# Decoder step on one core: the weight loads run eight products ahead instead of seven around one stage boundary

## The chip, the cores and the metric

The kernel runs on one core of one Trainium2 chip. The metric is the time of one execution in device microseconds; three runs of the kernel before gave 2320.79, 2322.99 and 2325.85 us, and the median, 2322.99 us, is its time.

## The reference, cut to what matters

Two layers of a hybrid decoder work on 1024 prompt tokens and 8 sample tokens of width 2048. The first layer is a pooling mixer, the second is sliding-window attention over one shared K/V. All products are in float32. Around the change the second layer is computed:

```python
k_p, v_p = shared_kv(xp, pos_p, w_kv)          # h @ w_kv, rotary on k
z = x @ w_in                                    # queries and gates
q = rope_partial(z[..., :D_ATTN].reshape(B, T, N_HEADS, HEAD_DIM), pos)
o = attn_core(q, kb, vb, q_pos, k_pos, sinks).reshape(B, T, D_ATTN)
y = (o * jax.nn.silu(gate)) @ w_out
return layer_norm(ALPHA * x + y, g_ln, b_ln)
```

## The kernel before, in words

**Stages.** The tokens are cut into two chunks of 512 and 520 columns. The table PHASES (lines 50 to 53) gives the order: input projection of layer one for both chunks, its output projection for both chunks, then `bi` for chunk 0 (fifth stage), `bi` for chunk 1 (sixth), `bo` for both chunks. A `bi` stage projects K/V and then, for eight pairs of heads, queries and gates, and does the attention in between.

**Products.** A projection of 256 output channels is done by Strassen's scheme as seven products of half size (`seven`, line 596). One product is 24 matmuls on TensorE (PE), lines 684 to 686: eight slices of weights, each as high part of the weights by high part of x, high by low, and low by high. So a product needs its weights as two tiles (high, low) and its x as two pairs of tiles. A pair of heads takes 14 products, seven for queries and seven for gates. In the K/V part two runs of seven go side by side (`both`, line 581), and two products in a row use the same x. At the start of a chunk 1 stage three extra matmuls (line 672) are issued first; their PSUM banks are those that the last pair of the stage before still holds.

**What a product costs the other engines.** A weight block (128x1024 float32, 512 KB) is loaded by SyncE (SP) in `load1` (line 285), rounded to its high part by ScalarE (ACT) in `cast_to` (line 505), and the low part is made by VectorE (DVE) in `prep_to` (line 520). Some blocks are sums of others: DVE adds (line 349), and GpSimd (POOL) stores the sum to HBM (line 351) for the second chunk. The x tiles of the next stage are loaded (line 828), cast (line 838) and subtracted (line 847) in the same way, one step of each after a product (`x_tick`). The results leave PSUM by copies of the next product's start (`posts`: lines 623 to 657; line 657 is the last copy of a pair). Attention adds per head: scores on PE (line 1874), a copy and a maximum (1891, 1895), eight exponentials (1910), eight scalings (1923), a transpose on PE (1927), two copies out (1936 on ACT, 1937 on DVE), values on PE (1951), the gate (1960) and its store by POOL (1963). Rotary needs the rows of the other half: four DMAs (`partner`, line 1728), two multiplications (1736) and an addition (1844), and the scores wait for that addition.

**What sets the order.** Everything is written in one stream. `begin` (line 532), called at each product, reads the triple `self.ahead`: weights are loaded up to `a` blocks ahead of the product, cast up to `b` ahead, and made low up to `d` ahead. It is (7, 4, 3) from the start. PE, DVE and ACT keep the order of the source; SP and POOL issue in an order that the tile scheduler chose when the program was built. All engines run in order, so an instruction that waits holds what stands behind it.

**Buffers.** `Mem` (line 139) hands out 54 slots, always the one that was freed longest ago; a slot whose contents are still being stored counts as ten releases younger. A tile is named m, slot, running number (m29_1955 is the 1955th tile, in slot 29). A load into a slot waits for the last reader of what was in it.

**`at(n, f)`** (line 570) runs f at the end of the n-th product from now. In `queries`, at the last pair of heads of chunk 1, `self.ahead` becomes (6, 4, 3), and in the seventh stage it goes back to (7, 4, 3).

Of the kernel before, what the change touches and what calls it, by code (L numbers as in the profile page):

```python
# [190 lines left out]
class Kern:  # L191
# [1918 lines left out]
    def phase_bi(self, c, ps, nxt):  # L2110
        nc = self.nc
        T = CHUNKS[c][1]
        if ps[0] == 0:
            self.kv_open(c)
        if not self.strassen:
            for done in (self.k_done, self.v_done):
                box = {}
                for j in range(2):

                    def take(ps, j=j, done=done, box=box):  # L2120
                        if j == 0:
                            box["s"] = self.mem.full(2 * T)
                        nc.scalar.copy(box["s"].a[:, j * T : (j + 1) * T], ps[:])
                        if j == 1:
                            done(c, box["s"])

                    self.unit(take)
            for t in range(2 * ps[0], 2 * ps[-1] + 2):
                def q_done(ps, t=t):
                    s = self.mem.half(T)  # L2130
                    nc.scalar.copy(s.a[:, :T], ps[:])
                    self.q_done(c, t, s, 1, 4)

                def g_done(ps, t=t):
                    s = self.mem.half(T)
                    nc.scalar.copy(s.a[:, :T], ps[:])
                    self.gate_done(c, t, s, 1)

                self.attend(c, t, 9, 13 if t <= 2 * ps[-1] else 8, 2)
                self.unit(q_done)  # L2140
                if t == 2 * ps[-1] - 1:
                    self.x_begin(nxt)
                self.last = t == 2 * ps[-1] + 1
                self.unit(g_done)
            self.last = False
            return
        if ps[0] == 0:
            pairs = []
            for done in (self.k_done, self.v_done):
                box, z0, z1 = self.two(T)  # L2150
                pairs.append((z0, z1, lambda done=done, box=box: done(c, box["s"])))
            self.both(c, *pairs)

        def queries(p):
            t0 = 2 * p
            if T > TP and p % 4 == 3:
                self.at(2, lambda p=p: self.dec_keys(p // 4))
            for n in range(2):
                t = t0 + n
                at, s1, ticks = (12 + 7 * n, {12: 11, 13: 9}.get(t, 12), SPREAD) if t < 14 else (  # L2160
                    11 + 7 * n, {14: 10, 15: 8}[t], CLOSE
                )
                self.attend(c, t, at, s1, 2, t > 12, ticks)
            if p == ps[-1]:
                self.x_begin(nxt)
                if c == 1:
                    self.ahead = 6, 4, 3
            box, z0, z1 = self.two(T)
            self.pair(c, z0, z1, lambda t0=t0, box=box: self.q_done(c, t0, box["s"], 2, 3))

        def gates(p):
            box, z0, z1 = self.two(T)

            def done():
                self.gate_done(c, 2 * p, box["s"], 2)
                if T > TP and p % 4 == 3:
                    self.decode(c, p // 4)

            self.last = p == ps[-1]
            self.pair(c, z0, z1, done)  # L2180

        for p in ps:
            queries(p)
            gates(p)
        self.last = False
# [296 lines left out]
```

## Time and profile before

| what | value |
|---|---|
| median of three runs | 2322.99 us |
| the profiled execution's own time | 2320.17 us |
| its span, first to last instruction | 2317.9 us |
| mean granted TensorE clock over the span | 0.997 |
| PE, DVE, ACT busy, share of the span | 99%, 84%, 60% |
| DMA over the span | 649.37 MB, 280 GB/s |

All times of the trace are microseconds from the start of the span, in the profiled execution. A row of a timeline has the start, the duration, the engine, the line in the kernel, the operation, the tiles (out<-in, without numbers), the shape and a count; a bracket at its end gives the engine's idle time ahead of it and what is believed to have ended it. SPq marks a DMA that SP issues: the row's duration is that of the issue, not of the transfer. A row of the view of waits has the waiting instruction, the one it waited for, the sum, the count and the longest.

### The profile page before, as it was taken

What the parts mean: (1) busy time and instruction counts of PE and PEld (TensorE: products, weight loads), DVE (VectorE), ACT (ScalarE), POOL (GpSimd) and SP (SyncE); (2) the same over time, 40 slices, a digit from 0 to 9 for tenths busy, and PEclk for the clock granted to TensorE, in tenths of its full rate; (3) what the DMA queues carried; (4) which work ended last, traced back from release to release, by engine and by line L of the source; (5) the groups of instructions that cost most, each with busy time, mean ns of one, the idle gap of its engine ahead of it and who ended that gap; (6) DMA issues with size and microseconds to landing.
All of it is one profiled execution on the core that took longest, in us unless ns stands there. A gap on an engine that the chain in (4) does not pass through costs nothing. (4 is left out here: it accounts for less than half of the span.)

```text
span 2317.9 us, 50529 instructions
## 1 busy us (share of the span) xinstructions
PE 2288.1 (99%) x20417; PEld 2217.7 (96%) x20417; DVE 1943.0 (84%) x2409; ACT 1389.3 (60%) x2548; POOL 191.1 (8%) x360
## 2 busy tenths in 40 slices
PE   9999999999999999999999999999999999999997
PEld 7999999999999999999889999989999999999997
DVE  8888889877878878988979898889877777889797
ACT  5544446544546547655566767685776678556565
POOL 0111110010000000000001111100000000000001
PEclk9999999999999999999999999999999999999999
DMA  7869679999989989999767666777787878799795
GB/s 261 287 242 315 229 245 330 315 309 303 304 302 322 335 284 333 317 392 345 245 234 241 233 234 236 252 259 250 234 252 240 252 230 288 251 360 381 252 330 184
DMA packets 246682, 649.37 MB, mean 280 GB/s; under 512 B 25232, under 2 KB 106032, under 8 KB 246448
## 3 DMA queue, kind: packets, MB, share of 16 engines
q1 hardware_dynamic: 204432, 493.66, 63.8%
q0 software_dynamic: 42016, 152.49, 17.0%
q8 instruction: 159, 2.61, 0.5%
q14 instruction: 75, 0.61, 0.1%
HBM read 463.54 MB, written 173.01 MB: 275 GB/s over the span
## 5 line engine op out<-in xcount | busy, mean ns | idle before, releaser
L684 PE MATMUL pD<-m,m 128*128 128x260 f32 (+1 forms) x5088 | 1441.3, 283 | 4.7 <-ACT pD L623 2.3
L686 PE MATMUL pD<-m,m 128*128 128x260 f32 (+1 forms) x5088 | 1434.7, 282 | 4.9 <-DVE m L520 4.9
L685 PE MATMUL pD<-m,m 128*128 128x260 f32 (+1 forms) x5088 | 1434.7, 282 | 0.0
L684 PEld LDWEIGHTS pD<-m,m 128*128 128x128 f32 x5088 | 959.4, 189 | 13.9 <-issue 6.2
L686 PEld LDWEIGHTS pD<-m,m 128*128 128x128 f32 x5088 | 959.8, 189 | 7.1 <-DVE m L520 7.0
L685 PEld LDWEIGHTS pD<-m,m 128*128 128x128 f32 x5088 | 959.1, 189 | 0.5
L520 DVE TENSOR_TENSOR m<-m,m 128x1024 fp32r<-128x1024 f32 x690 | 833.5, 1218 | 94.7 <-ACT m L505 44.1
L505 ACT CAST m<-m 128x1024 fp32r<-128x1024 f32 x690 | 720.5, 1049 | 249.9 <-DVE m L349 120.3
L349 DVE TENSOR_TENSOR m<-m,m 128x1024 f32<-128x1024 f32 x136 | 166.1, 1222 | 10.2 <-DMA m<-in_wia 5.7
L847 DVE TENSOR_TENSOR m<-m,m 128x1024 fp32r<-128x1024 f32 (+1 forms) x118 | 143.8, 1224 | 7.4 <-ACT m L838 5.8
L838 ACT CAST m<-m 128x1024 fp32r<-128x1024 f32 (+1 forms) x118 | 123.3, 1051 | 11.8 <-DVE m L520 3.5
L657 ACT COPY m<-pD 128x260 f32<-128x260 f32 (+1 forms) x89 | 33.2, 373 | 131.0 <-PE pD L686 131.0
L645 DVE TENSOR_TENSOR m<-pD,m 128x260 f32<-128x260 f32 (+1 forms) x92 | 38.4, 418 | 73.1 <-ACT pD L644 67.2
L1910 ACT ACTIVATE m<-m,sm 128x128 f32<-128x128 f32 x256 | 99.4, 392 | 0.0
L623 ACT ACTIVATE pD<-pD 128x260 f32<-128x260 f32 (+1 forms) x90 | 33.3, 370 | 102.2 <-PE pD L686 102.0
L1179 PE MATMUL pD<-m,m 128*128 128x260 f32 (+1 forms) x528 | 91.5, 323 | 0.0
L712 PE MATMUL pD<-m,m 128*128 128x512 f32 x224 | 89.1, 398 | 0.0
L714 PE MATMUL pD<-m,m 128*128 128x512 f32 x224 | 88.2, 394 | 0.0
L713 PE MATMUL pD<-m,m 128*128 128x512 f32 x224 | 88.1, 393 | 0.0
L1179 PEld LDWEIGHTS pD<-m,m 128*128 128x128 f32 x528 | 79.4, 188 | 8.2
L1923 ACT ACTIVATE m<-m,sm 128x128 f32<-128x128 f32 x256 | 81.8, 391 | 3.8 <-DVE sm L1918 3.4
L632 ACT COPY m<-pD 128x260 f32<-128x260 f32 (+1 forms) x92 | 34.3, 373 | 82.3 <-PE pD L686 82.0
(257 smaller groups left out, 2101.3 us busy)
## 6 DMA issues: line engine op xcount, KB each, us to landing
m<-in_wib SPq DMA_DIRECT2D x132, 512.0 KB
m<-in_wia SPq DMA_DIRECT2D x128, 512.0 KB
m<-swoa SPq DMA_DIRECT2D x64, 512.0 KB
swia<-m POOLq DMA_DIRECT2D x56, 512.0 KB, 4.9
m<-swia SPq DMA_DIRECT2D x56, 512.0 KB
m<-swob SPq DMA_DIRECT2D x56, 512.0 KB
m<-in_wob SPq DMA_DIRECT2D x52, 512.0 KB
m<-in_woa SPq DMA_DIRECT2D x48, 512.0 KB
```

The source lines that it names most:

```text
L349: self.nc.vector.tensor_add(s[out].a[:, :1024], s[x].a[:, :1024], s[y].a[:, :1024])
L505: self.nc.scalar.copy(hi.r[:, :1024], self.stream[self.cast].src().a[:, :1024])
L520: self.nc.vector.tensor_sub(lo.r[:, :1024], s.src().a[:, :1024], hi.a[:, :1024])
L684: nc.tensor.matmul(ps[:, :TH], wh[:, s], h, start=new and k == 0, stop=False, skip_group_check=on)
L685: nc.tensor.matmul(ps[:, :TH], wh[:, s], l, start=False, stop=False, skip_group_check=on)
L686: nc.tensor.matmul(ps[:, :TH], wl[:, s], h, start=False, stop=k == 7, skip_group_check=on)
L712: nc.tensor.matmul(ps[:], wh[:, s], h, start=par == 0 and k == 0, stop=False)
L714: nc.tensor.matmul(ps[:], wl[:, s], h, start=False, stop=par == 1 and k == 7)
L838: self.nc.scalar.copy(h.r[:, :n], s.a[:, :n])
L847: self.nc.vector.tensor_sub(l.r[:, :n], s.a[:, :n], h.a[:, :n])
L1179: nc.tensor.matmul(ps[:, : cs.stop - cs.start], ws[:, s], d[:, cs], start=f0 and k == 0, stop=l0 and k == 3,)
L1910: nc.scalar.activation(x["s3"][:, i, :], x["s3"][:, i, :], AF.Exp, bias=nm[:, i : i + 1], scale=0.125, accum_out=rs[:, i : i + 1],)
```

## The change

In `queries`, at the last pair of heads (p = 7), chunk 0 now also changes the triple: weights are loaded eight blocks ahead. It goes back to seven after 30 more products; 14 of these belong to the last pair, the others are the first of the sixth stage. Casts and low parts stay four and three ahead.

```diff
                 self.x_begin(nxt)
                 if c == 1:
                     self.ahead = 6, 4, 3
+                else:
+                    self.ahead = 8, 4, 3
+                    self.at(30, lambda: setattr(self, "ahead", (7, 4, 3)))
             box, z0, z1 = self.two(T)
```

No matmul, cast, copy or transfer is added or dropped. PE's rows are the same in the same order. What moves is the order of DMAs on SP and POOL, the slots that tiles get, and, in the sixth stage, the steps that sum the next weights (lines 453 to 459), most of them by a product or two.

The first place is SP's queue at the last pair of heads of the fifth stage, up to the first loads for the sixth. in_wib holds query and gate weights of this stage, in_wkv the K/V weights with which the sixth begins, h1 and th1 the x tiles of the sixth; L1728 are the four rotary DMAs of the last queries. Before:

```order
L285 DMA m29_1974_17956<-in_wib 128x1024
L828 DMA m19_1979_18002<-h1_95 128x4x260
L828 DMA m12_1989_18088<-th1_92 128x4x260
L1728 DMA m32_1977_17995<-m23_1962_17784 32x1024 x4
L828 DMA m1_1978_18000<-h1_95 128x4x260
L285 DMA m48_1980_18006<-in_wkv 128x1024
L828 DMA m50_1983_18044<-h1_95 128x4x260
L828 DMA m0_1984_18046<-h1_95 128x4x260
L285 DMA m14_1986_18050<-in_wkv 128x1024
L285 DMA m40_1990_18091<-in_wkv 128x1024
L285 DMA m20_1997_18136<-in_wkv 128x1024
```

and now:

```order
L285 DMA m43_1975_17958<-in_wkv 128x1024
L285 DMA m28_1970_17912<-in_wib 128x1024
L285 DMA m29_1991_18093<-in_wkv 128x1024
L828 DMA m19_1979_18002<-h1_95 128x4x260
L1728 DMA m5_1978_17997<-m46_1963_17786 32x1024 x4
L828 DMA m48_1980_18004<-h1_95 128x4x260
L285 DMA m33_1981_18008<-in_wkv 128x1024
L828 DMA m14_1984_18046<-h1_95 128x4x260
L828 DMA m39_1985_18048<-h1_95 128x4x260
L285 DMA m47_1987_18052<-in_wkv 128x1024
L828 DMA m40_1990_18090<-th1_92 128x4x260
```

Ahead of the rotary DMAs stood one weight load and two x tiles; now two K/V blocks (m43, m29), one block of gate weights and one x tile stand there. Of what follows them, the second K/V block (m14 before, m33 now) is the fifth transfer before and the second now.

The second place is ACT at the same boundary, from the first x cast of the sixth stage to the copy that ends the fifth stage (L657). Before:

```order
L838 CAST m17_1995_18132<-m1_1978_18000 128x1040
L638 COPY m43_1996_18134<-pD_329_17962 128x256
L505 CAST m52_1999_18140<-m48_1980_18006 128x1024
L838 CAST m41_2001_18219<-m19_1979_18002 128x1040
L644 COPY pD_329_17962<-pD_334_18004 128x256
L505 CAST m32_2005_18229<-m14_1986_18050 128x1024
L1923 ACTIVATE m39_1973_17952<-m39_1973_17952,sm_333_17991 128x128 x4
L1891 COPY m29_2006_18261<-pS_215_13088 128x768
L838 CAST m33_2008_18266<-m50_1983_18044 128x1040
L505 CAST m46_2012_18275<-m40_1990_18091 128x1024
L1923 ACTIVATE m39_1973_17952<-m39_1973_17952,sm_333_17991 128x128 x4
L838 CAST m31_2014_18315<-m0_1984_18046 128x1040
```

and now:

```order
L838 CAST m34_1996_18134<-m19_1979_18002 128x1040
L638 COPY m20_1997_18136<-pD_329_17964 128x256
L505 CAST m25_2000_18142<-m43_1975_17958 128x1024
L838 CAST m1_2002_18221<-m48_1980_18004 128x1040
L644 COPY pD_329_17964<-pD_334_18006 128x256
L505 CAST m28_2006_18231<-m33_1981_18008 128x1024
L1923 ACTIVATE m23_1974_17954<-m23_1974_17954,sm_333_17993 128x128 x4
L1891 COPY m50_2007_18263<-pS_215_13088 128x768
L838 CAST m2_2009_18268<-m14_1984_18046 128x1040
L505 CAST m9_2013_18277<-m47_1987_18052 128x1024
L1923 ACTIVATE m23_1974_17954<-m23_1974_17954,sm_333_17993 128x128 x4
L838 CAST m21_2015_18317<-m39_1985_18048 128x1040
```

The operations are the same in the same order (the L657 copy is the next row in both); only the slots differ. The cast of the second K/V block writes m32 before, a slot whose last reader was the rotary addition (L1844), and m28 now, where the seventh block of gate weights lay, read last by its own low part (L520).

The third place is SP at the end of the sixth stage. o0 and to0 are x tiles of the seventh stage, in_wob its weights. Before:

```order
L828 DMA m29_2529_23969<-o0_88 128x4x256
L828 DMA m39_2530_23971<-o0_88 128x4x256
L285 DMA m14_2524_23923<-swib15_140 128x1024
L1728 DMA m28_2527_23962<-m9_2510_23759 32x1040 x4
L285 DMA m42_2531_23975<-in_wib 128x1024
L2010 DMA out_nks<-m27_2506_23713 128x1024
L828 DMA m41_2535_24015<-o0_88 128x4x256
L828 DMA m49_2536_24017<-to0_85 128x4x256
L285 DMA m12_2538_24021<-in_wob 128x1024
L828 DMA m4_2541_24059<-to0_85 128x4x256
L285 DMA m35_2542_24062<-in_wob 128x1024
```

and now:

```order
L828 DMA m11_2533_23973<-o0_88 128x4x256
L828 DMA m52_2534_23975<-o0_88 128x4x256
L285 DMA m40_2528_23927<-swib15_140 128x1024
L285 DMA m23_2542_24025<-in_wob 128x1024
L1728 DMA m47_2531_23966<-m10_2514_23763 32x1040 x4
L285 DMA m53_2535_23979<-in_wib 128x1024
L2010 DMA out_nks<-m20_2510_23717 128x1024
L828 DMA m1_2539_24019<-o0_88 128x4x256
L828 DMA m12_2540_24021<-to0_85 128x4x256
L828 DMA m44_2545_24063<-to0_85 128x4x256
L285 DMA m48_2546_24066<-in_wob 128x1024
L285 DMA m3_2553_24112<-in_wob 128x1024
```

The first in_wob block has moved ahead of the four rotary DMAs; its slot (m23) is one whose contents, an attention output, POOL stores.

## The prediction

> **What bounds the kernel now.** First the page: who is busy.
>
> ```profile
> span 2317.9 us, 50529 instructions
> PE 2288.1 (99%) x20417; PEld 2217.7 (96%) x20417; DVE 1943.0 (84%) x2409; ACT 1389.3 (60%) x2548; POOL 191.1 (8%) x360
> ```
>
> PE is busy for 2288.1 of 2317.9 us, and the change takes no matmul away. All that it can win lies in the remaining 29.8 us and in busy time that runs at a lower clock. The view of PE's waits says where the 29.8 us are (waiting line, who ended the wait, sum, count, longest):
>
> ```profile
> PE pD L686 <- DVE m L520: 4.9, 9, 0.9
> PE pD L672 <- ACT m L657: 4.9, 1, 4.9
> PE pD L684 <- ACT m L657: 1.6, 1, 1.6
> ```
>
> The second row is the only long single wait: 4.9 us, once, at L672. That is the boundary of the fifth and sixth stages, the place of the change. PE's timeline there:
>
> ```profile
> 1506.40 0.28 PE L686 MATMUL pD<-m,m 128*128 128x256 f32 x1
> 1511.60 1.02 PE L672 MATMUL pD<-m,m 128*128 128x260 f32 x3 [4.92 <-ACT m L657]
> ```
>
> The fifth stage's last matmul ends at 1506.40 + 0.28 = 1506.68, the sixth stage's first starts at 1511.60: a stall of 4.92 us. The table of windows (length, PE, weight load, DVE, ACT, POOL busy with counts, granted clock, DMA share, GB/s) shows what follows:
>
> ```profile
> 1506.70:1511.60 4.90, 0.01 (x1) 0.01 (x1) 4.15 (x6) 4.87 (x10) 0.00 (x0) 0.90 1.05 386
> 1511.60:1517.60 6.00, 6.00 (x28) 6.00 (x29) 3.28 (x3) 4.57 (x12) 0.00 (x0) 0.51 1.05 389
> 1517.60:1520.00 2.40, 2.40 (x23) 2.40 (x22) 0.00 (x0) 2.25 (x4) 0.00 (x0) 1.00 1.07 382
> ```
>
> After the stall the clock is 0.51 for 6.00 us and then 1.00 again. At that clock 6.00 us hold 6.00 x 0.51 = 3.06 us of work, so the stall costs another 2.9 us.
>
> Why is ACT late with L657? Its own timeline before that copy:
>
> ```profile
> 1497.28 1.06 ACT L838 CAST m<-m 128x1040 fp32r<-128x1040 f32 x1 [2.66 <-DMA m<-h]
> 1504.33 1.05 ACT L505 CAST m<-m 128x1024 fp32r<-128x1024 f32 x1 [3.49 <-DVE m L1960]
> 1511.17 0.37 ACT L657 COPY m<-pD 128x256 f32<-128x256 f32 x1
> 1494.63:1511.17 16.54, 11.84 (x168) 11.00 (x166) 14.53 (x18) 10.39 (x18) 0.86 (x2) 0.98 1.05 373
> ```
>
> From 1494.63, the end of a head's last exponential, to 1511.17 ACT has 10.39 us of work (last row, a window) and two idles, 2.66 and 3.49 us. Without them L657 would start at 1511.17 - 6.15 = 1505.02, ahead of PE's last matmul. So the slack is 1506.68 - 1505.02 = 1.66 us. The first idle waits for an x tile's load. The second stands ahead of the cast of the second K/V block; the row names L1960, but that gate writes nothing the cast reads or overwrites. I take the block's load as the cause: it is one of the last in the queue that SP issued so:
>
> ```profile
> 1478.07 0.33 SPq L285 DMA_DIRECT2D m<-in_wib  x1
> 1480.71 0.38 SPq L828 DMA_DIRECT2D m<-h  x1
> 1487.73 0.38 SPq L828 DMA_DIRECT2D m<-th  x1
> 1488.20 3.11 SPq L1728 DMA_DIRECT2D m<-m  x4
> 1491.41 1.15 SPq L828 DMA_DIRECT2D m<-h  x1
> 1492.73 0.59 SPq L285 DMA_DIRECT2D m<-in_wkv  x1
> 1493.37 1.42 SPq L828 DMA_DIRECT2D m<-h  x2
> 1494.83 2.16 SPq L285 DMA_DIRECT2D m<-in_wkv  x3
> SPq L828 <- DMA o<-m: 6.4, 1, 6.4
> ```
>
> The th load waits 6.4 us for the store that still reads its slot (last row, SP's waits); the rotary DMAs and all loads stand behind it. The windows say what that does to the DMA engines:
>
> ```profile
> 1476.00:1482.00 6.00, 6.00 (x121) 5.55 (x121) 5.93 (x10) 3.03 (x7) 1.93 (x4) 1.00 0.53 188
> 1494.00:1500.00 6.00, 5.79 (x93) 5.41 (x94) 4.50 (x5) 3.34 (x8) 0.00 (x0) 1.00 1.06 324
> ```
>
> Half empty (0.53) until 1482, saturated (1.06) at 1494. The stall is bandwidth used late.
>
> **The change, part by part.** No instruction is added or removed, so every term is a moved wait.
>
> *The loads at the fifth stage's end.* Eight ahead instead of seven brings the first K/V block forward by one product, and slots are handed out otherwise. What the new slots wait for stands in these rows:
>
> ```profile
> 1472.44 0.53 POOL L351 DMA_DIRECT2D swib<-m  x1 [8.04 <-DVE m L349]
> 1478.87 1.21 DVE L520 TENSOR_TENSOR m<-m,m 128x1024 fp32r<-128x1024 f32 x1
> 1480.01 0.68 DVE L1960 SCALAR_TENSOR_TENSOR m<-pO,m 128x512 f32<-128x512 f32 x1
> 1482.30 0.37 ACT L657 COPY m<-pD 128x256 f32<-128x256 f32 x1 [0.68 <-PE pD L686]
> ```
>
> The first K/V block's slot m43 and the next block's m29 waited for stores or low parts that end by 1478.87 + 1.21 = 1480.08, and the first x tile's slot m19 for the gate, until 1480.69. The th load, with its 6.4 us wait, stands behind all of them and behind the rotary DMAs. Those need only their data, complete with L657 at 1482.67. So SP issues them at about 1482.8 instead of 1488.20, and what follows is about 5 us early, into the half-empty stretch. The second K/V block becomes the second transfer after the rotary DMAs instead of the fifth. So both of ACT's old idles go.
>
> A new wait takes their place. The second K/V block's cast now writes m28, which L520 of the last gate block reads last:
>
> ```profile
> 1495.81 2.36 DVE L1736 TENSOR_TENSOR m<-m,m 128x1024 f32<-128x1024 f32 x2 [1.46 <-DMA m<-m]
> 1499.35 1.22 DVE L520 TENSOR_TENSOR m<-m,m 128x1024 fp32r<-128x1024 f32 x1
> ```
>
> It ended at 1499.35 + 1.22 = 1500.57. DVE's own wait of 1.46 us for the rotary rows lies ahead of it; with them issued 5 us earlier it goes, and L520 ends at about 1499.11. Without idles ACT reaches that cast 6.15 us before 1504.33, at 1498.18. So it idles between 0.93 and 2.39 us, and L657 starts between 1505.95 and 1507.41, but not before PE's 1506.68. Behind the waiting cast stand all of ACT's casts and L657; PE waits for that. L672 follows 1511.60 - 1511.17 = 0.43 us behind L657: between 1507.11 and 1507.84. The stall shrinks by 4.49 to 3.76 us; because I expect DVE's wait to go, I take **4.4 us**.
>
> *The lower clock.* What is left is a gap of about half a microsecond. The 1.6 us wait above, at another boundary, is longer, and its surroundings show no reduced clock. So the 2.9 us go too: **2.9 us**, and 0 if a stall of several us stays.
>
> *What is late next.* DVE and ACT, early in the sixth stage, get 7 us less:
>
> ```profile
> 1517.75 0.37 ACT L623 ACTIVATE pD<-pD 128x260 f32<-128x260 f32 x1 [1.58 <-PE pD L686]
> 1520.00:1543.00 23.00, 23.00 (x262) 22.30 (x260) 22.81 (x27) 20.78 (x48) 1.39 (x3) 1.00 0.78 269
> ```
>
> ACT idled 1.58 us there waiting for PE, and DVE is full (22.81 of 23.00) but holds nothing up over those 23 us. Shifted earlier by 7 us, DVE's backlog becomes tight; I count no loss, and at worst 1 us (the sum of low-part waits over the whole kernel is 4.9 us in 9 pieces, 0.9 the longest).
>
> *The sixth stage's end.* There the first weight load of the seventh stage comes ahead of the rotary DMAs on SP, into slot m23, which still holds a row of outputs being stored:
>
> ```profile
> 1923.28 0.54 POOL L1963 DMA_DIRECT2D o<-m  x1 [23.79 <-DVE m L1960]
> DMA to landing us min/median/max: 5.8/5.8/5.8
> 1927.00 2.43 SPq L1728 DMA_DIRECT2D m<-m  x4
> 1939.71 2.38 DVE L1736 TENSOR_TENSOR m<-m,m 128x1040 f32<-128x1040 f32 x2
> 1942.12 1.24 DVE L1844 TENSOR_TENSOR m<-m,m 128x1040 f32<-128x1040 f32 x1
> 1943.63 1.32 PE L1874 MATMUL pS<-m,m 64*32 64x160 f32 x64
> 1952.50 0.39 PE L684 MATMUL pD<-m,m 128*128 128x256 f32 x1 [1.62 <-ACT m L657]
> ```
>
> The store lands at 1923.28 + 5.8 = 1929.1, so the load is issued then, and the rotary DMAs behind it at about 1929.6 instead of 1927.00: 2.6 us late, in parallel with 12.7 us (1927.00 to 1939.71) before DVE wants their rows. If the whole delay reached L1736, scores (L1874) would be late by 2.6 - 0.3, the 0.3 being 1943.63 - 1943.36, L1844's end. The 1.62 us that PE waits anyway at 1952.50 would absorb most of it. Bounds: -1 us, as the seventh stage's first weights now land earlier, and +3.2 us, a full delay with a push of the later casts as well. I take **+0.4 us**, near the row with 12.7 us of cover.
>
> *Sum*, against the profiled execution's own 2320.17 us: 2320.17 - 4.4 - 2.9 + 0.4 = 2313.3 us. The median of the three runs stands 2322.99 - 2320.17 = 2.8 us above that execution: **2316.1 us**. Best case of the forecast: -4.5 - 2.9 - 1.0 = -8.4, or 2314.6 by the median and 2311.8 if the new runs stand like the profiled one. Worst: -3.8 - 2.9 + 3.2 + 1.0 = -2.5, or 2320.5.
>
> **Rivals.** *The lower clock is not always there.* The mean clock of 0.90 over the 4.90 us of the stall means that about 0.1 x 4.90 / 0.49 = 1.0 us of it was at 0.51, so the clock fell some 4 us after PE had stopped, with 1 us of margin: a slightly shorter or otherwise placed stall misses it. If the timed runs before mostly missed it, only 4.0 us (4.4 - 0.4) are won: 2319.0 us. For it speaks that small margin; against it, that the one execution we see has it. The Trainium skill, "TensorE: Matmul & The Clock Gate", section "What's actually happening", says that the gate counts in free-running windows of 3.4 us and halves the clock after a window that is idle throughout. By that rule a stall of 4.92 us holds a whole window in only (4.92 - 3.41) / 3.41 = 0.44 of executions, an estimate, and this rival would be nearly even; the trace's reduced stretch, 1.0 + 6.0 = 7 us, agrees with two windows. One execution can't show how often it falls so.
>
> *The loads land no earlier.* The DMA share is 1.05 through the stall, so with more issued ahead each transfer takes longer and the late ones land when they did. Against it: the early stretch is at 0.53. Time: 2322.99 + 0.4, about 2323 us.
>
> *The sixth stage's end takes its full price:* -4.4 - 2.9 + 3.2 + 0.3 gives 2319.2 us.
>
> *Slower: a load that holds SP.* At the sixth stage's end the m23 load is the mechanism. Each microsecond that the store lands after 1929.1 delays the rotary DMAs, L1844 and, beyond the cover, PE by one; from a gap of about 4 us the clock falls too (+2.9). To undo 7.3 us it takes a gap of 4.4 + 2.9, so it turns slower from about 4.4 us of PE waiting there; a wait of 9 us gives -7.3 + 9 + 2.9 = +4.6, about 2328 us. Against it speaks the 5.8 us landing, a known store, and the 12.7 us cover.
>
> **How the numbers follow.** Forecast (2314.6 to 2318.3): 0.57, at 2316.1 us. Clock not reduced before: 0.13 at 2319.0. Full price at the second place: 0.08 at 2319.2. Loads no earlier: 0.14 at 2323. Slower: 0.08 at 2328. What a measurement of this kernel can tell from no change is about 0.2%, 4.6 us, so faster means under 2318.3 us. Faster gets the forecast and a little of its two near rivals (0.60), within 0.2% the rest of them and the unchanged loads (0.32), slower 0.08. The range runs from 2311.5, just under the best case of the new runs, to 2323.5, just over the unchanged loads; left out are the slow rival and a little on each side.
>
> **What would show it.** Right: on SP the rotary DMAs issued near 1482.8; ACT's idles of 2.66 and 3.49 us replaced by one of 1 to 2.4 us, ended by DVE's L520; L672 starting by 1507.9; the clock at 1.00 throughout 1506 to 1520; L1874 at most 1 us later, measured from the sixth stage's start. Wrong: an idle of over 3 us ahead of L657, a PE wait of over 2 us between the sixth and seventh stages, or new waits of PE for low parts (L520) early in the sixth stage, where the sums' steps now lie otherwise.

## The result, and the profile after

The changed kernel takes 2313.56 us in the median of 6 runs (2311.68 to 2317.01); the kernel before, run beside it, 2323.14 us (6 runs, 2319.91 to 2325.85). The ratio is 0.9962, with an interval of 0.9949 to 0.9975. In a later session the changed kernel gave 0.9964 (0.9952 to 0.9977). The forecast was 2316.1 us, a ratio of 0.997.

The profiled execution of the changed kernel took 2311.68 us. Its page, PE's waits, and PE at the fifth stage's end:

```profile
span 2309.7 us, 50525 instructions
PE 2286.1 (99%) x20417; PEld 2216.1 (96%) x20417; DVE 1943.4 (84%) x2409; ACT 1390.3 (60%) x2548; POOL 191.0 (8%) x360
```

```profile
PE pD L686 <- DVE m L520: 3.7, 9, 0.9
PE pD L684 <- ACT m L657: 1.3, 1, 1.3
PE pD L672 <- ACT m L657: 0.5, 1, 0.5
```

```profile
1506.43 0.62 PE L672 MATMUL pD<-m,m 128*128 128x260 f32 x3 [0.46 <-ACT m L657]
```

The one long wait of PE has shrunk from 4.92 to 0.46 us. The windows around it show the clock at 1.00 throughout, and DMA already busy before 1482 (0.79 where it was 0.53):

```profile
1506.00:1520.00 14.00, 13.57 (x127) 13.24 (x128) 12.91 (x15) 13.97 (x34) 0.00 (x0) 1.00 1.05 386
1476.00:1482.00 6.00, 6.00 (x123) 5.58 (x118) 5.93 (x10) 3.00 (x7) 1.93 (x4) 1.00 0.79 279
```

SP's queue shows why: the rotary DMAs start at 1482.31 instead of 1488.20, since no transfer ahead of them still waits when their own rows are ready, and the loads behind them follow 5 us earlier.

```profile
1479.74 0.33 SPq L285 DMA_DIRECT2D m<-in_wkv  x1
1480.34 0.55 SPq L828 DMA_DIRECT2D m<-h  x1
1482.31 3.74 SPq L1728 DMA_DIRECT2D m<-m  x4
1486.17 1.26 SPq L828 DMA_DIRECT2D m<-h  x1
1487.53 0.67 SPq L285 DMA_DIRECT2D m<-in_wkv  x1
```

On ACT the two idles of 2.66 and 3.49 us are gone. One of 1.01 us has come, at the cast of the second K/V block and ended by the low part L520, as forecast. L657 itself now waits for PE's last product, so the 0.46 us that are left are hardly more than the copy's own 0.37 us:

```profile
1498.60 1.05 ACT L505 CAST m<-m 128x1024 fp32r<-128x1024 f32 x1 [1.01 <-DVE m L520]
1506.00 0.37 ACT L657 COPY m<-pD 128x256 f32<-128x256 f32 x1 [0.45 <-PE pD L686]
```

To see where the time came from, the same PE instruction is looked up in both traces; the table has its start before, and how much earlier (-) it stands in the changed kernel. The first row is what the two executions differed by before the change can act.

| PE instruction | start before | first profile | second profile |
|---|---|---|---|
| scores L1874, fifth stage | 1453.9 | -0.38 | +0.01 |
| L672, sixth stage begins | 1511.6 | -5.17 | -4.78 |
| transposes L1927 just behind | 1517.6 | -7.68 | -7.29 |
| values L1951 | 1566.2 | -7.80 | -7.41 |
| scores L1874 | 1603.9 | -7.24 | -6.85 |
| scores L1874 | 1799.2 | -7.90 | -7.51 |
| scores L1874, the sixth stage's last products | 1943.6 | -7.39 | -6.86 |
| values L1951, seventh stage | 2005.6 | -7.70 | -7.52 |
| L672 of the last stage | 2127.6 | -9.08 | -8.82 |
| end of the span | 2317.9 | -8.2 | -7.9 |

So 4.8 us come at the stall, 2.5 us from the clock behind it, and the rest are steps of half a microsecond to both sides, one of 1.4 us in the seventh stage, and 0.9 us that are given back between 2127 and the end.

### The profile page after: what moved, and what is told of

It is laid out like the page before. It is cut to its first block, busy times and chain, and to the rows that moved or that the text cites. A ratio compares the mean times of both kernels' runs of the same rounds, so it can differ in the third digit from the quotient of the medians.

```text
span 2309.7 us, 50525 instructions
## 1 busy us (share of the span) xinstructions
PE 2286.1 (99%) x20417; PEld 2216.1 (96%) x20417; DVE 1943.4 (84%) x2409; ACT 1390.3 (60%) x2548; POOL 191.0 (8%) x360
## 5 line engine op out<-in xcount | busy, mean ns | idle before, releaser
L520 DVE TENSOR_TENSOR m<-m,m 128x1024 fp32r<-128x1024 f32 x690 | 834.1, 1219 | 92.6 <-ACT m L505 39.9
L657 ACT COPY m<-pD 128x260 f32<-128x260 f32 (+1 forms) x89 | 33.3, 374 | 131.3 <-PE pD L686 131.1
```

Of the source, the lines that this page charges most:

```text
L520: self.nc.vector.tensor_sub(lo.r[:, :1024], s.src().a[:, :1024], hi.a[:, :1024])
```

## The experiments

Theory A: what counts is SP's queue, where one load that waits for a store holds the rotary DMAs and all loads behind it. Theory B: what counts is that K/V blocks are loaded further ahead. The stall is measured as PE's idle ahead of L672.

**The kernel before again (e1).** The kernel is unchanged.

> The kernel before, unchanged, run again for its clock. If the reduced clock after the stall comes in every execution, the profile shows again some 6 to 7 us at 0.5 around 1511, and each run's mean clock is 0.997 like the first. If the stall meets the reduced clock only in some executions (the rival), about half of the runs have 0.998 and are some 2.5 us shorter than the others. Ratio 1.000 either way.

Measured: 0.9997 (0.9988 to 1.0005). The profile has the stall again and, behind it and at two other places, a reduced clock. PE's rows at these places, then the windows:

```profile
1512.22 1.02 PE L672 MATMUL pD<-m,m 128*128 128x260 f32 x3 [4.55 <-ACT m L657]
...
1952.13 0.40 PE L684 MATMUL pD<-m,m 128*128 128x256 f32 x1 [2.64 <-ACT m L657]
...
2271.69 0.39 PE L684 MATMUL pD<-m,m 128*128 128x260 f32 x1 [2.00 <-ACT m L632]
```

```profile
1512.05:1515.46 3.41, 3.24 (x15) 3.25 (x16) 3.41 (x4) 3.38 (x11) 0.00 (x0) 0.50 1.05 397
1952.37:1955.78 3.41, 3.41 (x18) 3.41 (x18) 3.41 (x4) 3.41 (x12) 0.00 (x0) 0.50 1.05 384
2273.22:2276.63 3.41, 3.41 (x18) 3.41 (x17) 1.82 (x4) 1.06 (x3) 0.00 (x0) 0.50 0.67 204
```

Even waits of 2.64 and 2.00 us were followed by half the clock. The mean clock of the 11 runs was 0.996 (7) or 0.997 (4), not 0.998 as in the first six runs of the changed kernel; of the 75 runs of the kernel before that stood beside the experiments, four had 0.998. The mean doesn't say where a run's reduced stretches lie. But all three profiles with the long stall (before, e1 and e3 below) have one right behind it, and by the figures in the last section a stall of over 3.8 us can't miss it. The rival that the timed runs mostly miss the reduced clock falls. What does vary is its length: two windows of 3.41 us before, only one in e1, where it cost 1.3 us and not 2.5.

**Eight ahead in the last pair only (e2), in the sixth stage only (e3).** The change's two halves:

```diff
 e2
-                    self.at(30, lambda: setattr(self, "ahead", (7, 4, 3)))
+                    self.at(14, lambda: setattr(self, "ahead", (7, 4, 3)))
 e3
-                    self.ahead = 8, 4, 3
+                    self.at(14, lambda: setattr(self, "ahead", (8, 4, 3)))
```

> Eight ahead only through the last pair of the fifth stage (14 products instead of 30). Theory A and B alike (the gain is made before the boundary): L672 starts within 0.3 us of its time in the changed kernel, 5 us earlier than before, no reduced clock, ratio 0.996 to 0.997. If the sixth stage's share of the change carried part of the gain, the ratio would lie nearer to 0.999.

> Eight ahead only from the end of the last pair on (the other 16 products). Theory A and B alike: the stall of 4.9 us and the reduced clock stay as before, ratio 0.999 to 1.001. If a longer lead in the sixth stage is worth something by itself, PE gains a microsecond or more after 1560.

Measured: e2 0.9983 (0.9974 to 0.9992), e3 0.9996 (0.9987 to 1.0005). At the stage boundary both did as expected: e2 has L672 at 1506.79 and no reduced clock, 7.3 us ahead behind it; e3 has the stall (4.30 us) and the reduced clock. But e2's ratio missed. It gives 2.5 us back between 1765 and 1800. There SP has a store of v rows (L2033) ahead of the rotary DMAs, and that store waits for a transfer. SP's waits and timeline, then DVE:

```profile
SPq L2033 <- DMA m<-m: 5.2, 4, 4.3
```

```profile
1775.98 0.34 SPq L2033 DMA_DIRECT2D out_nvs<-m  x1
1776.42 0.38 SPq L285 DMA_DIRECT2D m<-in_wib  x1
1776.91 2.65 SPq L1728 DMA_DIRECT2D m<-m  x4
```

```profile
1785.12 2.40 DVE L1736 TENSOR_TENSOR m<-m,m 128x1040 f32<-128x1040 f32 x2 [2.42 <-DMA m<-m]
```

In the changed kernel the rotary DMAs of that pair stand ahead of the store, at 1774.38, and DVE doesn't wait. So the sixth stage's half of the change brings nothing by itself (e3), but without it the queue falls out worse. e12 below tests the cause of this loss.

**Seven ahead with other slots (e4).** The slot rule is changed from the sixth pair of the fifth stage until the first pair of the sixth stage begins:

```diff
-        self.mem.release(self, 10 if stored else 0)
+        self.mem.release(self, self.mem.late if stored else 0)
...
+            if c == 0 and p == 5:
+                self.mem.late = 18
+            if c == 1 and p == 0:
+                self.mem.late = 10
```

> Weights stay seven ahead; only the rule for slots differs from the sixth pair of the fifth stage to its end: a slot still being stored counts as 18 releases younger instead of 10, so that the load of a th tile that waited for a store no longer stands ahead of the rotary DMAs. Theory A (the queue on SIO side is what counts, that is SP held by one load): the rotary DMAs are issued near 1483, ACT's idles of 2.66 and 3.49 us shrink to under 2.5 us together, the stall falls to under 1.5 us and the clock stays 1.00; ratio about 0.997. Theory B (weights have to be loaded earlier): the second K/V block is still late, the stall stays over 3 us, ratio 0.999 to 1.000.

("The queue on SIO side" in this text is SP's queue.) Measured: 0.9973 (0.9962 to 0.9984). With seven ahead the rotary DMAs start at 1482.93, and the stall is 1.29 us, with the clock at 1.00. SP, ACT and PE:

```profile
1482.93 5.29 SPq L1728 DMA_DIRECT2D m<-m  x4
```

```profile
1500.42 1.05 ACT L505 CAST m<-m 128x1024 fp32r<-128x1024 f32 x1 [2.34 <-DMA m<-in_wkv]
```

```profile
1507.69 0.51 PE L672 MATMUL pD<-m,m 128*128 128x260 f32 x2 [1.29 <-ACT m L657]
```

The middle row is the cast of the second K/V block, and its releaser is the block's load: what the 3.49 us before were taken for. Theory A explains most of the gain; B alone is refuted.

**Eight ahead, SP held (e5).**

```diff
             nc.gpsimd.dma_start(self.act["o", c][:, t, :TP], a.a[:, :TP])
+            if (c, t) == (0, 11): nc.sync.dma_start(self.dbg[:], self.act["o", c][:, t, :8])
```

> The changed kernel with one more DMA on SP just ahead of the rotary DMAs of the fifth stage's last queries: it copies 8 columns of the attention row that POOL stored last (8 floats on 128 rows), so it waits for that store, as the th load did before; slots and all other orders are those of the changed kernel. The rotary DMAs then start near 1487.5, 5 us later than in the changed kernel, and all loads behind them too. If the held queue alone makes the stall (theory A), it comes back to 4 us or more with the reduced clock, ratio 0.999 to 1.000. If only the earlier K/V block counts (theory B), the gap stays at 0.7 us, ratio 0.996. If both count, since two K/V blocks and an x tile are issued ahead of the hold here and only one x tile was before, the gap is 1 to 3 us and the ratio 0.997 to 0.999.

Measured: 0.9967 (0.9955 to 0.9979). The hold worked (the rotary DMAs start 1.1 us later than before), and the stall is 2.22 us, followed in the profiled execution by 3.41 us of half clock:

```profile
1488.70 0.50 SPq L1964 DMA_DIRECT2D dbg<-o  x1
1489.31 2.74 SPq L1728 DMA_DIRECT2D m<-m  x4
1492.79 0.49 SPq L285 DMA_DIRECT2D m<-in_wkv  x1
```

```profile
1508.37 0.63 PE L672 MATMUL pD<-m,m 128*128 128x260 f32 x3 [2.22 <-ACT m L657]
```

This is the middle case: with two K/V blocks ahead of the hold only 1.8 us of the 4.5 come back, and theory A alone is refuted too. By the numbers of their tiles the two are the first block and the fourth; the second, on whose cast ACT waited before, is issued at 1492.79 here, 2 us earlier than before, although the hold ends later. In times it can't be told from the changed kernel (0.9962 and 0.9964). The four stalls side by side: held and seven ahead 4.92, held and eight 2.22, not held and seven 1.29, not held and eight 0.46. Either cure takes most of the stall, so their gains don't add. Each figure is that of one execution; held and with seven ahead, e1 and e3 had 4.55 and 4.30 us.

**The stall filled with matmuls (e6).** The kernel before, with 36 unread matmuls behind the last product of the fifth stage:

```diff
+            if self.ph == "bi0" and self.last and idx == ORDER7[-1]:
+                o = self.pso.tile([P, 512], F32, tag="O", name=self.nm("pO"))
+                for _ in range(36):
+                    nc.tensor.matmul(o[:, :TH], wh[:, :P], h, start=True, stop=True)
```

> The kernel before with 36 matmuls more behind the last product of the fifth stage, into the pO bank that is free then; nobody reads them, and they wait for nothing that is late. They fill some 4.2 us of the stall on PE, while ACT's L657 and with it L672 stay where they are (near 1511.6). If the stall costs its 4.9 us and the reduced clock 2.5 to 2.9 us on top (forecast), the clock stays 1.00 there and what follows is 2.5 to 2.9 us earlier than before, ratio about 0.999. If the reduced clock costs nothing by itself, nothing moves after 1520, ratio 1.000.

Measured: 0.9986 (0.9978 to 0.9995). L672 stays where it was, and the clock stays at 1.00:

```profile
1512.00 0.63 PE L672 MATMUL pD<-m,m 128*128 128x260 f32 x3 [0.53 <-ACT m L657]
```

```profile
1506.70:1512.00 5.30, 4.77 (x42) 4.57 (x40) 4.75 (x7) 5.27 (x11) 0.00 (x0) 1.00 1.05 390
1512.00:1517.60 5.60, 5.60 (x46) 5.57 (x47) 3.31 (x3) 5.60 (x14) 0.00 (x0) 1.00 1.06 389
```

Against before, L672 stands +0.40 us and the transposes behind it -2.12 us: the reduced clock alone cost 2.5 us, the same as in the table above (7.68 - 5.17).

**Other slots at the sixth stage's end (e7).** The changed kernel, with the slot rule of e4 from `c == 1 and p == 5` to two products past the stage's end.

> The changed kernel with the slot rule (a slot still being stored counts as 18 releases younger, not 10) from the sixth pair of the sixth stage to two products past its end. No weight load that waits for a store stands ahead of that stage's last rotary DMAs any more. If the +0.47 us of the scores (L1874) there and the wait of 1.3 us behind them come from that hold, both shrink: L1874 back to the time it had, the stage boundary's wait under 1.3 us, 0.3 to 1 us won, ratio about 0.9960 against 0.9962 (not to be told apart by the times, so by the profile). If they come from something else, they stay.

Measured: 0.9973 (0.9963 to 0.9984). The scores L1874 lose nothing now (-6.86 us ahead of them and at them), so the 0.47 us did come from the held queue. But against the expectation the wait at the stage boundary grew, and a window of half the clock follows it, so that PE falls from -6.86 to -4.88 us against before:

```profile
PE pD L684 <- ACT m L657: 2.0, 1, 2.0
```

ACT's rows show why: the first in_wob block of the seventh stage, which in the changed kernel is issued at 1920.88 ahead of the rotary DMAs, is issued behind them at 1927.75 here, and its cast waits for it.

```profile
1935.84 1.05 ACT L505 CAST m<-m 128x1024 fp32r<-128x1024 f32 x1 [2.49 <-DMA m<-in_wob]
```

Nothing was won: what the early block costs the scores in the changed kernel it saves at the boundary. A wait of 0.64 us at 1840, which the changed kernel lacks, comes on top.

**Nine ahead (e8).** `self.ahead = 9, 4, 3` in place of 8.

> Nine ahead instead of eight, over the same 30 products. Theory A: no gain beyond eight at the boundary, since nothing waits there for weights any more (gap 0.7 us or more, more if the th load, which now stands ahead of the rotary DMAs again, waits for a store); with fewer free slots later waits may appear. Ratio 0.996 to 0.999. Theory B: gap under 0.7 us, ratio 0.995 to 0.996.

Measured: 1.0007 (0.9998 to 1.0015): all is lost again, a ratio outside both expectations. At the fifth stage's end SP is held once more (its rotary DMAs start at 1489.14) and the stall is 1.70 us, as theory A allowed for; at 1781 the rotary DMAs stand behind L2033 as in e2. DVE's wait behind that, what it makes of PE at 1796, and the clock:

```profile
1789.85 2.39 DVE L1736 TENSOR_TENSOR m<-m,m 128x1040 f32<-128x1040 f32 x2 [3.83 <-DMA m<-m]
```

```profile
PE pO L1951 <- ACT m L1936: 3.1, 1, 3.1
```

```profile
1796.10:1799.50 3.40, 2.77 (x26) 2.38 (x28) 3.13 (x6) 2.08 (x6) 0.00 (x0) 0.50 0.79 317
```

From 4.2 us ahead of before at 1772 it falls to 0.8 us behind at 1799. A wait of 3.31 us for a low part at 2096.98, again with half the clock behind it, adds to that; its cause was not followed.

**The changed kernel again (e9).** The kernel is unchanged.

> The changed kernel once more, for a second profile of it. If the terms read from its first profile are the kernel's and not one execution's: the gap at the fifth stage's end is 0.3 to 1 us again, the clock is 1.00 until the last stage's end, and the mean clock of the runs is 0.998, against 0.996 or 0.997 of the kernel before. Ratio 0.995 to 0.9975.

Measured: 0.9964; gap 0.46 us again, mean clock 0.998 in four of five runs. Its second profile is the last column of the table above: the steps agree within 0.4 us.

**Rotary DMAs issued by POOL (e10 to e12).** In `partner` of the kernel before, of the changed one, and of e2:

```diff
-            self.nc.sync.dma_start(t.a[32 * a : 32 * a + 32, : n * T], s.a[32 * b : 32 * b + 32, : n * T])
+            self.nc.gpsimd.dma_start(t.a[32 * a : 32 * a + 32, : n * T], s.a[32 * b : 32 * b + 32, : n * T])
```

> The kernel before, with all rotary DMAs (L1728) issued by POOL instead of SP. The th load still waits for its store and holds all x and K/V loads behind it, but no longer the rotary rows. If the held loads make the stall, it stays over 3.5 us (less at most the 1.46 us by which DVE waited for the rotary rows), with the reduced clock; ratio 0.998 to 1.000. If the held rotary rows make it, the gap falls to under 2 us; ratio 0.996 to 0.998.

Measured: 0.9979 (0.9970 to 0.9988), between the two cases. The th load still holds SP until 1488.73, but DVE no longer waits for rotary rows, and the loads behind no longer for the 3.11 us that SP spent on issuing the rotary DMAs. The stall is 2.91 us, the clock reduced for one window:

```profile
1495.25 2.35 DVE L1736 TENSOR_TENSOR m<-m,m 128x1024 f32<-128x1024 f32 x2
```

```profile
1510.31 0.63 PE L672 MATMUL pD<-m,m 128*128 128x260 f32 x3 [2.91 <-ACT m L657]
```

So of 4.92 us the held rotary rows and their issue make 2.0; another 2.5 (2.91 - 0.46) are left to the held loads and the late K/V blocks.

> The changed kernel with all rotary DMAs issued by POOL. At the fifth stage's end nothing is held any more, so the gap stays 0.3 to 1 us. At the sixth stage's end the rotary rows and the weight load behind them are no longer held by the load that waits for a store... the weight load still is. Ratio 0.995 to 0.998; below 0.9955 it would beat the changed kernel.

Measured: 0.9981 (0.9972 to 0.9990), just outside the expectation, and no better version. The stall stays at 0.46 us, but early in the sixth stage PE loses 2.66 us between 1604 and 1625 of the time before. 1.8 us of that are three waits for DVE. DVE itself had waited 3.44 us for rotary rows that POOL had issued from 1583.30 on, and was busy without a break from 1598 to 1603:

```profile
1593.75 2.39 DVE L1736 TENSOR_TENSOR m<-m,m 128x1040 f32<-128x1040 f32 x2 [3.44 <-DMA m<-m]
PE pD L686 <- DVE m L520: 1.1, 2, 0.6
PE pD L684 <- DVE m L650: 0.7, 1, 0.7
```

In the changed kernel, with SP issuing them at 1582.12, DVE waits for no rows there; why they come later by POOL was not followed. Another wait for a low part, 1.79 us at 2089.91, was followed by half the clock.

> Eight ahead through the last pair only (run e2, which lost 2.4 us between 1765 and 1797, where DVE waited 2.42 us for rotary rows), with all rotary DMAs issued by POOL. If that loss is rotary DMAs held on SP behind a store that waits, DVE's wait of 2.4 us goes and PE loses under 0.5 us between 1760 and 1800; ratio as the changed kernel's, 0.996 to 0.997, against 0.9983 of e2. If it comes from something else in the sixth stage's slots, the 2.4 us stay.

Measured: 0.9966 (0.9953 to 0.9978), against 0.9983 of e2, from which it differs only by the queue of all rotary DMAs. DVE's wait of 2.42 us is gone, and PE stands at -6.98 us at 1765 and -6.94 us at 1799, where e2 went from -7.52 to -4.98:

```profile
1783.17 2.38 DVE L1736 TENSOR_TENSOR m<-m,m 128x1040 f32<-128x1040 f32 x2
```

That the 2.5 us are lost to the rotary DMAs held on SP is thereby shown. The balance of zero hides a wait of 0.50 us at 1765.77, which e2 has as well (0.48 us), and one of 0.62 us at 1797 in the profile before, which e12 lacks.

## Why the prediction was right

**The stall.** 4.4 us were forecast, 4.46 came (4.92 to 0.46). The chain came out link by link: rotary DMAs at 1482.31 (forecast 1482.8), one new ACT idle of 1.01 us behind L520 (forecast 0.93 to 2.39), L672 at 1506.43 (forecast 1507.11 to 1507.84; 0.38 us of it are the executions' difference, and 0.34 us PE had gained on the way to the boundary). DVE's own wait of 1.46 us went, which decided for the early end. The prediction named both the freed queue and the K/V block's earlier place in it, without dividing the gain between them; e4 and e5 show that either alone takes most of it, 3.6 us the freed queue and 2.7 us the earlier K/V blocks. It took m29 for the next K/V block after the first; by the tiles' numbers it is the fourth, which changes no term of the sum. The rival that the loads land no earlier fell: the only idle of ACT that is left ahead of L657's own wait is ended by DVE, not by a load.

**The clock.** 2.9 us were forecast from the mean of a window, 2.5 came, in the changed kernel and in e6. Of the 6.83 us at half clock 5.87 lay behind L672's start; 2.5 us lost of them means that PE did 57% of its full rate's work, not 50%. The mechanism was right, the size 0.4 too large. Both figures belong to the execution that was profiled before, which had two windows at half clock; e1, the same kernel, had one, which cost 1.3 us. That the term fits so well is in part luck, and how often a run has one window or two is not known. The rival on the clock rested on a wrong reading, that it takes about 4 us of idling. e1 had it behind 2.0 us. So by the figures in the last section a stall of the size before meets it in every execution, and the changed kernel's gap of 0.46 us is far too short for it.

**What is late next.** Nothing was counted, 1 us at worst. Measured is 0.56 us, between 1566 and 1604 of the table, where PE waits for a low part that DVE makes too late:

```profile
1570.79 0.39 PE L686 MATMUL pD<-m,m 128*128 128x260 f32 x1 [0.23 <-DVE m L520]
```

Such waits were among the signs of being wrong; this one is small. It doesn't come from the shift by 7 us, as the prediction feared: e2 is shifted by 7.3 us and loses nothing there, and e3, which isn't shifted, loses 0.54 us. It comes with the sixth stage's half of the change.

**The sixth stage's end.** +0.4 us were forecast, +0.2 came in the first profile and nothing in the second: L1874 0.5 us later (0.65 in the second), 0.3 (0.66) given back by the boundary's wait (1.62 to 1.31 and 1.01 us). So the rival of the full price did not come. The hold was as computed (the store's landing puts the rotary DMAs 2.2 us late in the shifted time), but its way to PE was another. SP, ACT, DVE and PE of the changed kernel:

```profile
1920.88 0.35 SPq L285 DMA_DIRECT2D m<-in_wob  x1
1921.32 2.42 SPq L1728 DMA_DIRECT2D m<-m  x4
1923.83 0.54 SPq L285 DMA_DIRECT2D m<-in_wib  x1
```

```profile
1929.39 1.05 ACT L505 CAST m<-m 128x1024 fp32r<-128x1024 f32 x1 [1.68 <-DMA m<-in_wib]
1930.35 1.01 ACT L1936 COPY m<-pS 128x1024 f32<-128x1024 f32 x1
```

```profile
1931.39 1.23 DVE L1937 TENSOR_TENSOR m<-pS,cst 128x1024 f32<-128x1024 f32 x1 [4.23 <-ACT m L1936]
1932.53 2.38 DVE L1736 TENSOR_TENSOR m<-m,m 128x1040 f32<-128x1040 f32 x2
```

```profile
1936.24 1.32 PE L1874 MATMUL pS<-m,m 64*32 64x160 f32 x64 [0.40 <-DVE m L1844]
```

DVE has the rotary rows in time (no wait at L1736). Late is the in_wib block that SP issues behind them: its cast waits 1.68 us (0.97 before), and ACT's copy L1936, DVE and the scores stand behind that cast. The prediction had weighed the DMAs held, and not the load that is held behind them.

**What was not in the sum.** 1.4 us come between 2005 and 2127: PE's two waits for low parts there (0.66 us at 2030 and 0.88 at 2094 before) are one of 0.3 us in both profiles of the changed kernel. The first of them is no gain of the change: e1, the kernel before, doesn't have it either, though its second is 1.51 us. Why the second is short in the changed kernel was not followed. The 0.6 us at 1799 are no gain of the change either: in e1 that wait of 0.62 us at 1797 is absent too. In sum the traces' spans differ by 8.2 us, of which 0.4 lay ahead of the change and 1.3 are these two waits, which come and go between executions of the kernel before. In the medians it is 9.6 us in one session and 6.5 in the other; the single runs of each kernel spread over 4.5 to 7 us. So the times can't tell a forecast of 6.9 us from one that is two microseconds off; that the terms are right rests on the traces.

**The slower rival** did not come in the changed kernel. With nine ahead (e8) its mechanism did, at another place: rotary DMAs on SP behind a transfer that waits, 3.1 us of PE, and half the clock behind that.

## What to carry to other kernels

Where a queue issues in order, look first for the one entry that waits (here a load whose slot a store still read) and at all that stands behind it, also the innocent loads; a longer lead is worth what it changes in that order, and one step more (nine) can lose all of it. A boundary that stalls for several microseconds costs more than the wait, since the clock falls behind it; price both, and see whether filler work on the engine would save the second part. Compare two executions of the same kernel before reading half microseconds out of a trace.

## What the runs showed of the hardware

The clock's transitions lie on a grid of 3.41 us: every reduced stretch within the stages was 3.41 or 6.83 us long. With that grid laid over PE's rows of all fourteen profiles, a window at full clock in which PE stood idle for 1.88 us or more was always followed by half the clock, one with 1.69 us or less never. Some of these windows (the idle is worked out from the gaps between PE's rows):

| kernel | window from | idle of 3.41 us | clock of the next |
|---|---|---|---|
| before | 1950.96 | 1.53 | 1.0 |
| e1 | 1498.40 | 1.69 | 1.0 |
| e11 | 2087.32 | 1.79 | 0.5 |
| e5 | 1939.07 | 1.83 | 1.0 |
| e1 | 2269.81 | 1.88 | 0.5 |
| e3 | 1951.59 | 2.03 | 0.5 |
| e7 | 1943.80 | 2.04 | 0.5 |
| e10 | 1508.17 | 2.13 | 0.5 |
| e8 | 2093.06 | 2.80 | 0.5 |

Between 1.79 and 1.83 it went either way, so a little over half a window decides. In a window already at half the clock less was enough to stay there: 0.95 us of idle (before, from 1510.64) and 1.56 us (e3, from 1511.27) were followed by a second one, 0.63 us or less never. The Trainium skill, "TensorE: Matmul & The Clock Gate", section "What's actually happening", names an idle window as the condition; here windows that were busy for 1.5 us met it too, and the measurement decides. One reduced window cost PE 1.3 to 1.5 us in e1, two cost 2.5 us before. By these figures a wait of under about 1.7 us is safe by itself, and one of over 3.8 us never is, since at least 1.88 us of it lie in one window. Between them the place on the grid decides: e1's 2.00 us at 2271.69 was followed by half the clock, e8's 2.21 us at 1954.09 was not.
